# Dilated attention scores: from three split passes over both heads to one float32 matmul per head, and queries and keys written directly in class order

## The chip, the cores and the metric

The kernel runs on one core of a Trainium2 chip. The metric is the device time of one launch in microseconds (us). Before the change the median of three runs is 1536.92 us (1534.99 to 1537.64).

The engines are named as the profile names them: PE is TensorE's matmuls, PEld its weight loads, DVE is VectorE, ACT is ScalarE, POOL is GpSimd, SP is the queue from which nearly all DMAs are issued. PE writes its results to PSUM, which the program uses as eight banks of 128 x 512 float32; the other engines read them there. A line number such as L939 is a line of the kernel before, if nothing else is said.

## What is computed

An encoder block over 1024 tokens of width 1024: one input projection, three mixers side by side, a merge, an output projection. The change touches one mixer, the dilated window attention. It has 24 heads of width 64, in three groups `g` of eight heads; a group has a dilation `DIL[g]` of 1, 4 or 16.

```
def dilated_window_attention(q, k, v, window, dilation):
    half = window // (2 * dilation)          # 64, 64, 64
    qg, kg, vg = regroup(q), regroup(k), regroup(v)   # positions sorted by their class mod dilation
    ...
    sc = jnp.einsum('znqhd,znkhd->znhqk', qb, kw) * (dh ** -0.5)
    sc = jnp.where(valid[None, :, None], sc, NEG_INF)   # |qpos - kpos| <= 64, in the same class
    m = jnp.max(sc, axis=-1, keepdims=True)
    p = jnp.exp(sc - m)
    l = jnp.sum(p, axis=-1, keepdims=True)
    o = jnp.einsum('znhqk,znkhd->znqhd', p / l, vw)
    lse = m + jnp.log(l)
```

Queries and keys get rotary positions first. The outputs of the three groups are added up with weights softmax(lse).

## The kernel before

**Whole program.** PE's order is written out by hand. `weave` puts two streams together: the matmuls of dense projections (`dense`, 24 matmuls for half a unit of 128 output channels x 512 tokens, in three terms L143, L145, L147, because a float32 product is made from split operands: hi*hi, lo*hi, hi*lo), and the steps of an attention generator. After each step it goes on with the stream that is behind, by costs in ns that the code gives (216 for a dense matmul; an attention step yields its own). The totals that pace the attention are `A_COST`. On DVE, ACT, POOL and SP a scheduler sets the order from dependences and priorities; attention steps have the higher priority. An engine works off its queue in that fixed order.

**Stage of the dilated attention** (`with tc.tile_pool(name="aa")`). There are twelve visits, one for each head pair `p_` (0 to 3) and group `g` (0 to 2). Each visit (`a_att`) runs woven into three dense units: queries, keys and values of the visit after it (`add_a`). The last visit runs woven into three units of another stage. A unit's result comes in two halves in two PSUM tiles `d` (there are two such banks for the whole program), and has to be taken out of them before the half after next can start on PE.

Taking them out, for queries and keys (`rope_half`, L832 to L838): three DVE multiplications with the cosine and sine tables `tab` into `rot` and `t2a`, then one POOL addition. After the second half the keys or queries are split: `aqh` by ACT and `aql` by DVE for queries (L105, L106); for keys, one copy for each of the two heads in which the other head's rows are zero (`C_KM`), `akh` by ACT (L862) and `akl` by DVE (L863). The tokens are sorted into classes in these splits (`class_view`, `cls`). For values (L879) DVE writes the sorted classes at once, and POOL copies the class ends (L885).

**One visit**, with eight query tiles `T` of 128:

- transposes of the values (L913), brought to SBUF by ACT (L915)
- `scores(T)`: three matmuls (`passes`, L125) of one query tile against both heads' keys, the heads side by side in one PSUM bank (`s`, two banks); `n` is the key window, 128, 192 or 256 columns for a head. For each head DVE adds the mask and takes the minimum (L939), and ACT makes the exponential and its sum (L942 to L947)
- `trans(T)`: three, four or two transposes of the exponentials (L965, L974) into one PSUM tile `tr` (two banks), brought to SBUF by ACT (`app`, L977)
- `pv(b)`: for four tiles, the product with the values (L989), in plain float32, each head's 64 columns on its own half of the array's columns, into `ov` (two banks); ACT brings it out (`og`, L998)
- at the end the minima and sums are transposed and stored (`sts`, `sr`, `std`)

`scores(T)` is followed by `trans(T - 2)`, and `pv` comes three tiles behind. After the three groups of a head pair, `combine` makes the weights (`ceg`, `wgd`, `wgt`) and multiplies the three `og` by them (L1083); its five steps are called at given tiles of the next visits (`STEP_T`) and are placed behind that tile's last score operation on DVE (`issue_after`).

## Time and profile before

| | |
|---|---|
| median of 3 runs | 1536.92 us |
| profiled execution | 1537.39 us, span 1535.6 us |
| mean granted TensorE clock | 0.993 |
| PE, PEld busy | 1498.6, 1238.4 us |
| DVE, ACT, POOL busy | 972.8, 712.7, 443.9 us |
| stage of the dilated attention | 585 to 1151 us of the span: 566 us |
| in that stage PE, DVE, ACT, POOL busy | 563.1, 328.8, 282.9, 121.5 us |

An engine's busy time is the time in which at least one of its instructions runs. PE's matmuls overlap: a record of 0.39 us can start 0.23 us after the one before it, so PE's rate is read from the distance of starts. In a view by windows a row has, for each engine, the busy time and, behind it in brackets, the number of instructions, and then the granted clock, the DMA share and GB/s. In a view of groups a row has line, engine, operation, tiles, shape, count, then busy us and mean ns, then the idle time before it and who ended it.

### The profile page before, as it was taken

What the parts mean: (1) busy time and instruction counts of PE and PEld (TensorE: products, weight loads), DVE (VectorE), ACT (ScalarE), POOL (GpSimd) and SP (SyncE); (2) the same over time, 40 slices, a digit from 0 to 9 for tenths busy, and PEclk for the clock granted to TensorE, in tenths of its full rate; (3) what the DMA queues carried; (4) which work ended last, traced back from release to release, by engine and by line L of the source; (5) the groups of instructions that cost most, each with busy time, mean ns of one, the idle gap of its engine ahead of it and who ended that gap; (6) DMA issues with size and microseconds to landing.
All of it is one profiled execution on the core that took longest, in us unless ns stands there. A gap on an engine that the chain in (4) does not pass through costs nothing.

```text
span 1535.6 us, 20807 instructions
## 1 busy us (share of the span) xinstructions
PE 1498.6 (98%) x7748; PEld 1238.4 (81%) x7748; DVE 972.8 (63%) x1598; ACT 712.7 (46%) x1457; POOL 443.9 (29%) x363
## 2 busy tenths in 40 slices
PE   6999989999999999999999999999999999999998
PEld 5899977777777778888878888887888788888787
DVE  7765469989988985555566466556625442524843
ACT  5453346676666662554446445444642111212321
POOL 4415512444544552211221222122200100233422
PEclk9999999999999999999999999999999999999999
DMA  5332011111112112101121121112126441523332
GB/s 211 95 126 70 29 42 62 56 42 62 53 41 63 62 56 93 41 29 42 45 68 42 42 80 47 42 31 83 42 76 194 164 132 35 204 70 117 124 110 96
DMA packets 55044, 119.79 MB, mean 78 GB/s; under 512 B 13792, under 2 KB 23712, under 8 KB 54816
## 3 DMA queue, kind: packets, MB, share of 16 engines
q1 hardware_dynamic: 54800, 118.34, 23.4%
q8 instruction: 61, 1.00, 0.3%
q14 instruction: 39, 0.32, 0.1%
q10 hardware_dynamic: 144, 0.13, 0.0%
HBM read 96.06 MB, written 22.38 MB: 77 GB/s over the span
## 4 chain that ended last, share of the span: by engine, by line
PE 75%; DVE 11%; issue 4%; ACT 3%; DMA 3%; POOL 2%; SPq 0%; DVEq 0%; POOLq 0%; ACTq 0%
PE d L147 12%; PE d L143 12%; PE d L145 12%; PE sc L125 7%; PE sc L1248 4%; PE s L125 3%; PE sc L147 3%; PE sc L145 3%; PE sc L143 3%; PE ov L989 2%; DVE bpl L106 2%; PE s L709 1%; DVE bn L691 1%; PE ov L730 1%; PE s L708 1%
## 5 line engine op out<-in xcount | busy, mean ns | idle before, releaser
L143 PE MATMUL d<-hh,wh 128*128 128x512 f32 x992 | 396.1, 399 | 1.4 <-DVE fth L222 1.4
L147 PE MATMUL d<-hh,wl 128*128 128x512 f32 x992 | 397.2, 400 | 0.0
L145 PE MATMUL d<-hl,wh 128*128 128x512 f32 x992 | 393.6, 397 | 0.0
L147 PEld LDWEIGHTS d<-hh,wl 128*128 128x128 f32 x992 | 187.1, 189 | 38.5 <-issue 3.6
L143 PEld LDWEIGHTS d<-hh,wh 128*128 128x128 f32 x992 | 187.2, 189 | 38.3 <-DVE fth L222 2.3
L145 PEld LDWEIGHTS d<-hl,wh 128*128 128x128 f32 x992 | 187.1, 189 | 36.2 <-issue 1.0
L105 ACT ACTIVATE wh<-wr 128x1024 fp32r<-128x1024 f32 (+1 forms) x100 | 95.4, 955 | 246.7 <-PE sc L145 108.3
L720 POOL TENSOR_TENSOR bl<-bl,bp 128x512 f32<-128x512 f32 x96 | 135.5, 1412 | 120.4 <-ACT bp L711 112.1
L838 POOL TENSOR_TENSOR rot<-rot,t2a 128x512 f32<-128x512 f32 x48 | 82.6, 1721 | 297.4 <-DVE t2a L837 297.4
L106 DVE TENSOR_TENSOR bpl<-bp,bph 128x512 fp32r<-128x512 f32 x128 | 130.5, 1020 | 23.8 <-ACT bph L105 23.3
L106 DVE TENSOR_TENSOR wl<-wr,wh 128x1024 fp32r<-128x1024 f32 (+1 forms) x100 | 119.0, 1191 | 21.2 <-ACT wh L105 20.5
L1149 POOL TENSOR_TENSOR acc<-acc,th 128x1024 f32<-128x1024 f32 x16 | 45.4, 2837 | 203.8 <-DVE th L1148 203.8
L711 ACT ACTIVATE bp<-s 128x512 f32<-128x512 f32 x128 | 76.2, 595 | 60.0 <-PE s L709 58.2
L947 ACT ACTIVATE pra<-pra,sts 128x128 f32<-128x128 f32 (+2 forms) x152 | 67.2, 443 | 61.9 <-DVE sts L939 61.2
L147 PE MATMUL sc<-hh,wl 128*128 128x512 f32 x224 | 87.8, 392 | 1.8 <-DVE wl L106 1.8
L691 DVE TENSOR_REDUCE bn<-tr 128x1 f32<-128x512 f32 x128 | 86.7, 681 | 4.4 <-PE tr L690 3.9
L143 PE MATMUL sc<-hh,wh 128*128 128x512 f32 x224 | 87.9, 392 | 0.0
L145 PE MATMUL sc<-hl,wh 128*128 128x512 f32 x224 | 87.9, 392 | 0.0
L939 DVE CUSTOM_DVE_ANT_0 pra<-s,mask 128x128 f32<-128x128 f32 (+2 forms) x152 | 48.4, 348 | 61.8 <-PE s L125 49.1
L105 ACT ACTIVATE bph<-bp 128x512 fp32r<-128x512 f32 x128 | 80.9, 632 | 3.5
L835 DVE TENSOR_TENSOR rot<-d,tab 128x512 f32<-128x512 f32 x48 | 33.1, 690 | 67.5 <-PE d L147 67.2
L125 PE MATMUL sc<-gh,wh 128*128 128x512 f32 x192 | 74.7, 389 | 0.0
(278 smaller groups left out, 3096.9 us busy)
## 6 DMA issues: line engine op xcount, KB each, us to landing
wr<-in_wu SPq DMA_DIRECT2D x76, 512.0 KB
g2d<-fth SPq DMA_DIRECT2D x24, 256.0 KB
wgt<-wgd SPq DMA_DIRECT2D x24, 256.0 KB
ot<-od SPq DMA_DIRECT2D x12, 512.0 KB
gt<-g2d SPq DMA_DIRECT2D x12, 512.0 KB
wr<-in_wbr SPq DMA_DIRECT2D x24, 256.0 KB
thd<-fth SPq DMA_DIRECT2D x20, 256.0 KB
th<-thd SPq DMA_DIRECT2D x10, 512.0 KB
```

Source lines behind the costliest of these rows:

```text
L105: A.activation(dst_h, src, AF.Copy)
L106: V.tensor_tensor(dst_l, src, dst_h.bitcast(F32), op=OP.subtract)
L125: PE.matmul(out_ps, a, b, start=i == 0, stop=i == n - 1)
L143: PE.matmul(dst, wh[:, k, :], hh[k][:, t], start=k == 0, stop=False)
L145: PE.matmul(dst, wh[:, k, :], hl[k][:, t], start=False, stop=False)
L147: PE.matmul(dst, wl[:, k, :], hh[k][:, t], start=False, stop=k == 7)
L691: V.tensor_reduce(st[i]["n"][:, j, c:c + 1], s, axis=AX.X, op=OP.min)
L711: A.activation(pp, s, AF.Exp, scale=-1.0)
L720: G.tensor_tensor(lsum[i % 2], lsum[i % 2], pp, op=OP.add)
L838: G.tensor_tensor(o[:, t], o[:, t], t2, op=OP.add)
L947: A.activation(src, raw, AF.Exp, scale=-1.0, bias=bias, accum_out=sts[:, h, 1, T:T + 1])
L1248: PE.matmul(parts[h], *terms[h][j], start=j == 0, stop=j == 23)
```

## The change

1. The split and the zeroed copies of queries and keys go. `qk_evac` writes one float32 tile for queries (`aq`) and one for keys (`ak`), each with two buffers, already in class order: `rope_half` reads PSUM and tables through the strided view `classes`. The scale -0.125 goes into the query's multiplications (`scalar_tensor_tensor` in place of `tensor_tensor`).
2. The channel order of the weights is the plain one (`layout`), so the sine part of `rope_half` is four multiplications on 32 partitions, where there were two on 64.
3. `scores` is one float32 matmul for each head, on 64 rows of the array: head 0 on rows 0 to 63, head 1 on rows 64 to 127, each into its own PSUM bank. One call does four query tiles; a visit calls it twice.
4. PSUM: four banks for scores, one for `tr`, one for `ov` (before: two, two, two).
5. The order of the attention's steps: `scores(0)` first, then for each tile 300 ns of dense work and `trans(T)`; the second `scores` before tile 2, the first `pv` before tile 5. `A_COST` is new. The steps of `combine` are placed behind the last multiplication that takes a `d` tile out (`fp["last"]`).

```diff
-    phase_psum("ps_a", s1=2, t=2, o=2)
+    phase_psum("ps_a", s1=4, t=1, o=1)
...
+        def half_of(ap, half, g):
+
+            if g == 0:
+                return ap[:, half * 512:half * 512 + 512]
+            n = S // DIL[g] // 2
+            return ap.rearrange("p (r u) -> p r u", r=DIL[g])[:, :, half * n:half * n + n]
+
+        def classes(ap, g):
+            return ap if g == 0 else ap.rearrange("p (u r) -> p r u", r=DIL[g])
...
-        def rope_half(o, half, p):
+        def rope_half(o, half, p, scale, g):
             t = slice(half * 512, half * 512 + 512)
             t2 = aa.tile([P, 512], F32, name="t2a", bufs=2)
-            V.tensor_tensor(o[:, t], p, tab[:, 0, t], op=OP.mult)
-            V.tensor_tensor(t2[0:64], p[64:128], tab[64:128, 1, t], op=OP.mult)
-            V.tensor_tensor(t2[64:128], p[0:64], tab[0:64, 1, t], op=OP.mult)
-            G.tensor_tensor(o[:, t], o[:, t], t2, op=OP.add)
+            cos, sin = [classes(tab[:, i, t], g) for i in range(2)]
+            p = classes(p, g)
+            dst = half_of(o, half, g)
+            tmp = t2 if len(p.shape) == 2 else t2.rearrange("p (r u) -> p r u", r=DIL[g])
+
+            def mult(out, x, y):
+                if scale is None:
+                    return V.tensor_tensor(out, x, y, op=OP.mult)
+                return V.scalar_tensor_tensor(out, x, scale, y, op0=OP.mult, op1=OP.mult)
+
+            mult(dst, p, cos)
+            for a in range(4):
+                i, j = slice(32 * a, 32 * a + 32), slice(32 * (a ^ 1), 32 * (a ^ 1) + 32)
+                fp["last"] = mult(tmp[i], p[j], sin[j])
+            G.tensor_tensor(dst, dst, tmp, op=OP.add)
...
-            def q_evac(half, p):
...
-                if half == 1:
-                    d["q"] = (aa.tile([P, S], R, name="aqh", bufs=2), aa.tile([P, S], R, name="aql", bufs=2))
-                    split(cls(d["q"][0], g), cls(d["q"][1], g), class_view(d["rot"], g))
...
-                    for h in range(2):
-                        mc = cs[:, C_KM + h:C_KM + h + 1]
-                        A.activation(cls(kh[:, h], g), ov, AF.Copy, scale=mc)
-                        V.scalar_tensor_tensor(cls(kl[:, h], g), ov, mc, cls(kh[:, h], g).bitcast(F32),
-                                               op0=OP.mult, op1=OP.subtract)
+            def qk_evac(name, scale):
+                def evac(half, p):
+                    if half == 0:
+                        d[name] = aa.tile([P, S], F32, name=f"a{name}", bufs=2)
+                    rope_half(d[name], half, p, scale, g)
+                return evac
...
-            def scores(T):
-                lo, hi, mo = window(g, T)
-                n = hi - lo
-                sv = pss1().rearrange("p (h k) -> p h k", h=2)[:, :, :n]
-                qs = slice(T * 128, T * 128 + 128)
-                passes(sv, [(qh[:, qs], kh[:, :, lo:hi]), (qh[:, qs], kl[:, :, lo:hi]), (ql[:, qs], kh[:, :, lo:hi])])
-                pr = aa.tile([P, 512], F32, name="pra", bufs=4)
+            def scores(b):
+                svs, cost = [], 0
+                for j in range(4):
+                    T = 4 * b + j
+                    lo, hi, mo = window(g, T)
+                    n = hi - lo
+                    if j % 2 == 0:
+                        banks = [pss1(), pss1()]
+                    sv = [x[:, j % 2 * 256:j % 2 * 256 + n] for x in banks]
+                    for h in range(2):
+                        hs = slice(h * 64, h * 64 + 64)
+                        PE.matmul(sv[h], span(qa[hs], T * 128, T * 128 + 128, g), span(ka[hs], lo, hi, g),
+                                  start=True, stop=True)
+                    svs.append((T, n, mo, sv))
+                    cost += 4 * n / 2.4
+                for T, n, mo, sv in svs:
+                    pr = aa.tile([P, 512], F32, name="pra", bufs=6)
...
-            for T in range(NT + LA_P):
-                if T < NT:
-                    cost = scores(T)
-                    if todo and T == STEP_T[-len(todo)]:
-                        with tc.issue_after(last["dve"].ins):
-                            todo.pop(0)()
-                    yield cost
-                if 0 <= T - LA_T < NT:
-                    yield trans(T - LA_T)
-                if T >= LA_P and (T - LA_P) % 4 == 3:
-                    yield pv((T - LA_P) // 4)
+            yield scores(0)
+            for T in range(NT):
+                if todo and T == STEP_T[-len(todo)]:
+                    with tc.issue_after(fp["last"].ins):
+                        todo.pop(0)()
+                if T == 2:
+                    yield scores(1)
+                if T == 5:
+                    yield pv(0)
+                yield 300
+                yield trans(T)
+            yield 300
+            yield 300
+            yield pv(1)
...
-        A_COST = (13200.0, 11800.0, 8000.0)
+        A_COST = (15300.0, 14300.0, 10500.0)
...
-            units.append(unit(b + pair))
-            units.append(unit(1536 + b + pair))
-            units.append(unit(3072 + b + np.arange(128)))
+            units += [unit(1536 * j + b + np.arange(128)) for j in range(3)]
```

More of the change, by code (lines that the diff above doesn't have):

```diff
@@ L21 @@
 DIL = (1, 4, 16)
-C_ID, C_KM, C_GP, C_GM, C_BM, C_END = 0, 128, 130, 138, 146, 426
+C_ID, C_GP, C_GM, C_BM, C_END = 0, 130, 138, 146, 426
 B_COS, B_SIN, B_QN, B_QS, B_KN, B_KS = 0, 512, 170, 234, 298, 362
@@ L818, in block, with span @@
         G.tensor_tensor(tab[:, 1], tab[:, 1], rb, op=OP.mult)
-        def class_view(ap, g):
+        def half_of(ap, half, g):
             if g == 0:
-                return ap
-            return ap.rearrange("p (u r) -> p r u", r=DIL[g])
-        def cls(ap, g):
-            if g == 0:
-                return ap
-            return ap.rearrange("p (r u) -> p r u", r=DIL[g])
+                return ap[:, half * 512:half * 512 + 512]
[3 more added lines that the diff above has]
+            return ap if g == 0 else ap.rearrange("p (u r) -> p r u", r=DIL[g])
+        def span(ap, lo, hi, g):
+            return ap[:, lo:hi]
         OPS = {}
-        def rope_half(o, half, p):
+        def rope_half(o, half, p, scale, g):
             t = slice(half * 512, half * 512 + 512)
             t2 = aa.tile([P, 512], F32, name="t2a", bufs=2)
-            V.tensor_tensor(o[:, t], p, tab[:, 0, t], op=OP.mult)
-            V.tensor_tensor(t2[0:64], p[64:128], tab[64:128, 1, t], op=OP.mult)
-            V.tensor_tensor(t2[64:128], p[0:64], tab[0:64, 1, t], op=OP.mult)
-            G.tensor_tensor(o[:, t], o[:, t], t2, op=OP.add)
+            cos, sin = [classes(tab[:, i, t], g) for i in range(2)]
[11 more added lines that the diff above has]
+            G.tensor_tensor(dst, dst, tmp, op=OP.add)
         def add_a(p_, g):
@@ L842, in add_a @@
             d = OPS[p_, g] = {}
-            def q_evac(half, p):
-                if half == 0:
-                    d["rot"] = aa.tile([P, S], F32, name="rot", bufs=1)
-                rope_half(d["rot"], half, p)
-                if half == 1:
-                    d["q"] = (aa.tile([P, S], R, name="aqh", bufs=2), aa.tile([P, S], R, name="aql", bufs=2))
-                    split(cls(d["q"][0], g), cls(d["q"][1], g), class_view(d["rot"], g))
-            def k_evac(half, p):
-                if half == 0:
-                    d["rot"] = aa.tile([P, S], F32, name="rot", bufs=1)
-                rope_half(d["rot"], half, p)
-                if half == 1:
-                    kh = aa.tile([P, 2, S], R, name="akh", bufs=1)
-                    kl = aa.tile([P, 2, S], R, name="akl", bufs=1)
-                    ov = class_view(d["rot"], g)
-                    for h in range(2):
-                        mc = cs[:, C_KM + h:C_KM + h + 1]
-                        A.activation(cls(kh[:, h], g), ov, AF.Copy, scale=mc)
-                        V.scalar_tensor_tensor(cls(kl[:, h], g), ov, mc, cls(kh[:, h], g).bitcast(F32),
-                                               op0=OP.mult, op1=OP.subtract)
-                    d["k"] = (kh, kl)
+            def qk_evac(name, scale):
[4 more added lines that the diff above has]
+                return evac
             def v_evac(half, p):
@@ L878, in v_evac @@
                     p, rv = [v.rearrange("p (u r) -> p r u", r=r) for v in (p, rv)]
-                V.tensor_tensor(dst, p, rv, op=OP.mult)
+                fp["last"] = V.tensor_tensor(dst, p, rv, op=OP.mult)
                 if half == 1 and g < 2:
@@ L885, in v_evac @@
                             G.tensor_copy(vd[hs, e, :DIL[g], h], src)
-            units = [(base, q_evac), (base + 1, k_evac), (base + 2, v_evac)]
+            units = [(base, qk_evac("q", -0.125)), (base + 1, qk_evac("k", None)), (base + 2, v_evac)]
             for u, evac in units if base else units[::-1]:
@@ L893, in a_att @@
             d = OPS.pop((p_, g))
-            qh, ql = d["q"]
-            kh, kl = d["k"]
-            vt = d["vt"]
+            qa, ka, vt = d["q"], d["k"], d["vt"]
             for _ in range(4):
@@ L920, in a_att @@
             sts = cb.tile([P, 2, 2, NT], F32, name="sts", bufs=2)
-            st, last = {}, {}
+            st = {}
             def blocks_of(T):
@@ L925, in blocks_of @@
                 return [(i, c - lo, m) for i, (c, m) in enumerate(blocks) if lo <= c < hi]
-            def scores(T):
-                lo, hi, mo = window(g, T)
-                n = hi - lo
-                sv = pss1().rearrange("p (h k) -> p h k", h=2)[:, :, :n]
-                qs = slice(T * 128, T * 128 + 128)
-                passes(sv, [(qh[:, qs], kh[:, :, lo:hi]), (qh[:, qs], kl[:, :, lo:hi]), (ql[:, qs], kh[:, :, lo:hi])])
-                pr = aa.tile([P, 512], F32, name="pra", bufs=4)
-                for h in range(2):
-                    src = pr[:, h * n:h * n + n]
-                    bias = sts[:, h, 0, T:T + 1]
-                    moved = n == 192 and (h == 0) == (blocks_of(T)[0][2] == 64)
-                    raw = sv[:, h] if moved else src
-                    last["dve"] = V.tensor_tensor_reduce(raw, sv[:, h], mask[:, mo:mo + n], 1.0, 3.0e38, OP.add, OP.min, bias)
-                    if moved:
-                        a, b = (64, 0) if h == 0 else (0, 128)
-                        A.activation(src[:, h * 64:h * 64 + 128], raw[:, a:a + 128], AF.Exp, scale=-1.0, bias=bias,
-                                     accum_out=sts[:, h, 1, T:T + 1])
-                        A.activation(src[:, 128 - h * 128:192 - h * 128], raw[:, b:b + 64], AF.Exp, scale=-1.0, bias=bias,
-                                     accum_out=lx[:, h, T:T + 1])
-                    else:
-                        A.activation(src, raw, AF.Exp, scale=-1.0, bias=bias, accum_out=sts[:, h, 1, T:T + 1])
-                st[T] = pr
-                return 3 * n * 0.84
@@ new lines, in scores @@
+            def scores(b):
[15 more added lines that the diff above has]
+                    pr = aa.tile([P, 512], F32, name="pra", bufs=6)
+                    for h in range(2):
+                        src = pr[:, h * n:h * n + n]
+                        bias = sts[:, h, 0, T:T + 1]
+                        moved = n == 192 and (h == 0) == (blocks_of(T)[0][2] == 64)
+                        raw = sv[h] if moved else src
+                        V.tensor_tensor_reduce(raw, sv[h], mask[:, mo:mo + n], 1.0, 3.0e38, OP.add, OP.min, bias)
+                        if moved:
+                            a, c = (64, 0) if h == 0 else (0, 128)
+                            A.activation(src[:, h * 64:h * 64 + 128], raw[:, a:a + 128], AF.Exp, scale=-1.0, bias=bias,
+                                         accum_out=sts[:, h, 1, T:T + 1])
+                            A.activation(src[:, 128 - h * 128:192 - h * 128], raw[:, c:c + 64], AF.Exp, scale=-1.0,
+                                         bias=bias, accum_out=lx[:, h, T:T + 1])
+                        else:
+                            A.activation(src, raw, AF.Exp, scale=-1.0, bias=bias, accum_out=sts[:, h, 1, T:T + 1])
+                    st[T] = pr
+                return cost
@@ L1305, in unit @@
         return w[:, cols].reshape(8, P, 128).transpose(1, 0, 2)
-    i32 = np.arange(32)
-    pair = np.concatenate([i32, 64 + i32, 32 + i32, 96 + i32])
     units = []
@@ L1343, in layout @@
     r['msk'] = m
-    lane = np.arange(128) // 32 % 2
-    cst[:, C_KM] = np.where(lane == 0, -0.125, 0.0)
-    cst[:, C_KM + 1] = np.where(lane == 1, -0.125, 0.0)
     cst[:, C_GP:C_GP + 8] = inp['g_pre'][0].reshape(8, P).T
@@ L1361, in layout @@
         tab[q * 32:q * 32 + 32, 0] = ca.T
-        tab[q * 32:q * 32 + 32, 1] = sa.T if q < 2 else -sa.T
+        tab[q * 32:q * 32 + 32, 1] = -sa.T if q % 2 else sa.T
     r['tabA'] = tab
```

## The prediction

> **What bounds the kernel now.** The page first: PE is busy for 98% of the span, and PE's three dense lines lead the chain of work that ended last. The view by windows cuts out the stage that is changed; then the groups (every shape apart) and the timeline of that stage.

> ```profile
> PE 1498.6 (98%) x7748; PEld 1238.4 (81%) x7748; DVE 972.8 (63%) x1598; ACT 712.7 (46%) x1457; POOL 443.9 (29%) x363
> ...
> PE d L147 12%; PE d L143 12%; PE d L145 12%; PE sc L125 7%; PE sc L1248 4%; PE s L125 3%; PE sc L147 3%; PE sc L145 3%; PE sc L143 3%; PE ov L989 2%; DVE bpl L106 2%; PE s L709 1%; DVE bn L691 1%; PE ov L730 1%; PE s L708 1%
> ```

> ```profile
> 585.00:1151.00 566.00, 563.11 (x3180) 461.10 (x3179) 328.77 (x692) 282.85 (x698) 121.53 (x87) 1.00 0.17 53
> ```

> In 566 us PE idles 2.9. DVE (328.8 busy) and ACT (282.9) have room on average, but each works in order: it matters when they are late. Starts of PE in one piece of the timeline:

> ```profile
> 642.64 0.40 PE L143 MATMUL d<-hh,wh 128*128 128x512 f32 x1
> 642.97 1.97 PE L989 MATMUL ov<-app,avs 128*64 128x128 f32 x32
> 644.87 0.50 PE L145 MATMUL d<-hl,wh 128*128 128x512 f32 x1
> 645.21 0.40 PE L147 MATMUL d<-hh,wl 128*128 128x512 f32 x1
> ...
> 649.35 0.33 PE L125 MATMUL s<-akh,aqh 128*128 128x384 f32 x1
> 649.52 0.34 PE L125 MATMUL s<-akl,aqh 128*128 128x384 f32 x1
> ```

> The reader is to see the distances: dense matmuls stand 0.228 apart elsewhere in this stage, a 384-column score matmul costs 0.17, and the plain float32 product has two records for each matmul, and its 32 records start in 16 pairs, 0.109 a pair for 128 columns: the two heads, on two halves of the array, run at once. From 642.64 to 645.21 are 2.57 us; less two dense ones (0.456) and 16 x 0.109 (1.744), 0.37 is left for going into the split array and out.

> **The change, part by part**, against the profiled execution's 1537.4 (span 1535.6 and 1.8 around it; 0.5 over the median).

> *Scores on PE.* Before: 96 tiles x 3 passes at 0.23 (24 tiles of 512 columns), 0.173 (40 of 384), 0.116 (32 of 256): 48.6 us. After: the windows of one head sum to 24x256 + 40x192 + 32x128 = 17,920 columns; at the pair's rate, two passes of 0.109 per 128 columns for both heads, 30.5 us. 24 calls at 0.37 add 8.9. Row halves are nowhere in this trace; between both heads at once and one after the other I take at once, by the nearest row (the column halves), and for the switch the same row; the ends are 30.5 and 69.9. Net **-9.2**.

> *Removed copies.* `aqh`, `akh` take 63.6 off ACT, `aql`, `akl` 64.2 off DVE; nothing of it is on PE.

> *Taking queries and keys out of PSUM.* Five DVE operations for a half instead of three, and for g = 1, 2 strided. The values are already taken out so:

> ```profile
> L879 DVE TENSOR_TENSOR vta<-d,rb x24: 684/1063/1098, 586.2 to 1112.2; 128x512 f32<-128x512 f32 x24
> ```

> Its eight plain ones take 0.69, its sixteen strided ones 1.04 to 1.10. With 0.015 between operations (rope before: 0.705 from start to start at 0.69) a strided half costs 5 x 1.085 = **5.4 us** of DVE, a plain one 3.5; before it was 2.1. Sum: 16 x 3.5 + 32 x 5.4 - 48 x 2.1 = +128, less the 64 removed: DVE goes from 329 to some 393 in the stage. That scaling the query costs nothing more is by L222 (a scalar_tensor_tensor, 685 ns against 680). A half must be out before the half after next starts; a half is 5.5 us on PE, 7 with attention. So DVE is now just short of PE's pace and everything else in its queue pushes a half back. No row has 32 partitions strided: the ends are a plain 0.705 and 1.1; L836 on 64 partitions (693 ns), L835 on 128 (690) and L699 on 4 (689) cost the same, so I take 1.085.

> *POOL's additions* stay 48 at 1.28 to 2.33 us, 5.4 apart at the least: hidden. *Query scale in channels, constants*: nothing.

> *Bunched scores, one `tr` bank.* The order of the changed program on each engine says who stands behind whom. ACT: all exponentials of tiles 4 to 7, then `app` of tile 2. PE: the transposes of tile 3 need the only `tr` bank, hence that `app`. Before, exponentials came a tile at a time and there were two banks. I walk the three kinds of visit with the rows.

> Visit of g = 1 (queries and keys of g = 2 woven in), from the end of the queries' first half. DVE: hand-over 0.25, first half 5.4, eight L939 at 0.40 from start to start 3.2, second half 5.4, eight more 3.2, among them a weight split 1.35: 18.8; ACT's last exponentials and `app` 1.5: 20.3. PE until tile 3's transposes: 49 dense matmuls 11.2, two score calls 3.3, three transpose calls 1.3: 15.8. **PE waits 4.5.** For p_ >= 1 a multiplication by the weights (L1083, 2.02) stands in the same DVE stretch: 6.5 in two pieces (2.2 before the third tile of the second score call, whose banks tile 3 of the first still holds).

> Visit of g = 0: the same walk ends 0.7 late at the second half of the keys for p_ = 0. For p_ >= 1 ACT's `ceg` stands between the exponentials and `app`, and waits for DVE's small operations behind a weight split: 2.5 more, 3.2.

> Visit of g = 2: plain halves, 3.5 each, and L939 at 0.22: nothing.

> Sum 4.5 + 3 x 6.5 + 0.7 + 3 x 3.2 = **+34.3**. Off go three stalls of now (a transpose and a product waiting for `app`, 1.2 together per p_ >= 1): -3.5. If the cover were whole (0) or DVE slower, the ends are 0 and 45.

> *The clock.* A long wait costs once more:

> ```profile
> 1194.00:1195.00 1.00, 1.00 (x4) 0.76 (x5) 1.00 (x2) 0.00 (x0) 0.00 (x0) 0.63 0.28 41
> 1195.00:1196.00 1.00, 1.00 (x4) 0.81 (x3) 1.00 (x1) 0.00 (x0) 0.00 (x0) 0.50 0.88 348
> ```

> This follows PE starts 2.18 us apart (1191.65 to 1193.84); the clock (third number from the end) is 0.5 and the matmuls stand 0.43 apart for 3.4 us, 1.7 lost. A distance of 1.66 (at 419) cost nothing. I take 1.7 for each of the four waits over 4 us: **+6.8**; the three of 2.5 are too near the limit to count, ends 0 and 7 x 3.4. [...]

> *Moved steps.* `combine`'s DMAs go behind the last `d` multiplication: on SP a 512 KB weight load now stands before `wgd` instead of after the first `wgt`; it feeds a unit two ahead, and SP's own longest wait is for weight splits (158.6 us in this stage), so nothing, at most 1 us per head pair. `A_COST` equals the new steps' sum within 2%: attention and dense work still end together.

> Sum: 1537.4 - 9.2 - 3.5 + 34.3 + 6.8 = 1565.8, **1566**.

> **The rivals.** *Faster: DVE keeps up.* Place: the ten operations of two query halves in each g = 1 visit. If 32 partitions strided cost 0.705, that chain is 3.8 shorter, the waits shrink to 0.7 and 2.7, g = 0's to about 0, no clock is lost: 1537.4 - 9.2 - 3.5 + 8.8 = 1533.5, and 1525 if the switch costs nothing too. It decides below about 0.75 an operation. Against it: L879 has the same views.
> *Row halves one after the other.* Scores cost 30.5 more; in the visits of g = 1 (2.6 each) and three of g = 0 (1.6 of 3.3) that comes out of the waits: 1566 + 30.5 - 10.4 - 5 = 1581. For it: no row of this trace has two row halves at once.
> *Weight loads bind.* A score tile needs four loads of 128 columns. The 256-column passes show one such load per 0.116; four of these in a row are 0.46, against 0.22, 0.33, 0.44 by the pair's rate for 128, 192, 256 columns: 32 x 0.25 + 40 x 0.14 + 24 x 0.03 = 14.3, of it 4.5 inside g = 1's waits: 1576. [...] Against it: L989's loads start in pairs.
> *No change in work done*: not open, the copies are gone from the order.

> **How the numbers follow.** Forecast (1545 to 1580 by the ends of waits and clock) 0.50; DVE keeps up 0.25; row halves serial 0.13; weight loads 0.12. The range leaves out half of the fast case's lower part and little above: 1527 to 1586. A measurement of this kernel tells 0.2% (3 us) from no change. Slower: the three slow cases, less a little of the first, 0.72; within 0.2% 0.06; faster 0.22.

> **What the profile after would show.** DVE near 393 busy in the stage, strided 32-partition operations near 1070 ns; PE's score records in pairs, some 1.6 us a call for g = 0; PE waiting for ACT `app` once in each visit of g = 1; granted clock dipping there. Wrong if those operations are near 700 ns, if PE has no such waits, or if single score records follow one another at full length.

## The result and the profile after

The changed kernel takes 1559.68 us in the median of 4 runs (1557.76 to 1560.97), beside 1536.64 for the kernel before: 1.0156 times, so 1.6% slower, 95% interval 1.0144 to 1.0169. A second measurement (experiment 6) gave 1.0145 (1.0128 to 1.0163). The forecast was 1566, the range 1527 to 1586. The profiled execution took 1560.97 (span 1559.2) at a mean granted clock of 0.986. Line numbers from here on are those of the changed kernel; an experiment that adds lines has its own.

The page of the changed kernel, engines and the chain that ended last:

```profile
PE 1501.5 (96%) x7844; PEld 1226.9 (79%) x7844; DVE 1029.4 (66%) x1658; ACT 652.8 (42%) x1421; POOL 442.1 (28%) x363
...
PE d L143 12%; PE d L147 12%; PE d L145 12%; PE sc L125 7%; PE sc L1257 4%; DVE t2a L846 3%; PE sc L147 3%; PE sc L143 3%; PE sc L145 3%; PE ov L995 2%; DVE bpl L106 2%; PE ov L730 1%; PE s L709 1%; PE s L934 1%; PE s L708 1%
```

A new engine stands in the chain: DVE with `t2a`, the sine part of `rope_half`. The stage of the dilated attention (view by windows; columns as in the section on the profile before):

```profile
585.00:1175.00 590.00, 568.04 (x3284) 451.21 (x3283) 385.32 (x752) 223.90 (x662) 119.93 (x87) 0.98 0.17 51
```

ACT lost 59 us of work, DVE gained 57, and PE, which idled 2.9 us in 566, idles 22. The stage starts where it did, and the first matmul behind it, of tile `sc`, starts at 1175.38 in place of 1153.22: 22.2 us of the loss lie in the stage. From there to the end of the span are 383.8 us, 382.3 before; in experiment 6 they are 380.9, so this part differs from one execution to the next.

**What a score call costs PE** (timeline of PE, a call of g = 0):

```profile
618.79 0.47 PE L147 MATMUL d<-hh,wl 128*128 128x512 f32 x1
619.19 1.89 PE L934 MATMUL s<-ak,aq 64*128 64x192 f32 x16
621.01 0.50 PE L143 MATMUL d<-hh,wh 128*128 128x512 f32 x1
```

From the first of the 16 records to the next dense start are 1.82 us. The records start in pairs, 0.006 to 0.007 us apart, one of each head, and a pair of 256 columns takes 0.215 from start to start: both row halves work at once.

**What taking queries and keys out costs DVE** (the tile `t2a`; ns are least, median, greatest):

```profile
L845 DVE TENSOR_TENSOR t2a<-d,tab x96: 679/1021/1087, 597.9 to 1124.8; 32x512 f32<-32x512 f32 x96
L846 DVE SCALAR_TENSOR_TENSOR t2a<-d,tab x96: 679/1027/1100, 608.7 to 1106.8; 32x512 f32<-32x512 f32 x96
```

By group the medians are 687 ns (plain), 1057 (dilation 4) and 1022 (dilation 16). The values, with the same strided views, are where they were:

```profile
L877 DVE TENSOR_TENSOR vta<-d,rb x24: 691/1058/1084, 586.3 to 1134.7; 128x512 f32<-128x512 f32 x24
```

**Whom PE waits for** (view of waits, 580 to 1180; total us, times, longest):

```profile
PE tr L971 <- ACT app L983: 11.3, 5, 3.0
PE tr L980 <- ACT app L983: 8.2, 3, 2.7
PE d L143 <- DVE t2a L846: 1.8, 4, 0.5
```

Measured by the distances of PE's starts, these are 13 gaps with 23.7 us over the usual 0.23. Six of them are 3.1 to 3.4 us long, one in each visit of g = 0 and g = 1 with p_ >= 1. One of the kind in g = 1, in the timeline:

```profile
811.66 0.35 ACT L948 ACTIVATE pra<-s,sts 128x128 f32<-128x128 f32 x1
...
812.07 1.03 DVE L846 SCALAR_TENSOR_TENSOR t2a<-d,tab 32x512 f32<-32x512 f32 x1
...
813.09 0.40 PE L147 MATMUL d<-hh,wl 128*128 128x512 f32 x1
813.13 1.92 DVE L1092 TENSOR_TENSOR og<-og,wgt 128x1024 f32<-128x1024 f32 x1
...
815.08 0.36 DVE L945 CUSTOM_DVE_ANT_0 pra<-s,mask 128x192 f32<-128x192 f32 x1
...
815.48 0.45 ACT L953 ACTIVATE pra<-pra,sts 128x192 f32<-128x192 f32 x1 [2.01 <-DVE sts L945]
...
815.93 0.47 ACT L983 ACTIVATE app<-tr 128x384 f32<-128x384 f32 x1
...
816.46 0.90 PE L971 MATMUL tr<-cs,pra 128*128 128x128 f32 x3 [2.97 <-ACT app L983]
```

Read it from below. PE wants the transposes of tile 1; the only `tr` bank still holds tile 0. Its copy `app` was possible from 812 on, but ACT's queue has the exponentials of the four tiles ahead of it, all but those of the last head. The last of them waits 2.01 us for DVE's mask operation, and DVE is busy with a strided multiplication and then with `combine`'s weighting (L1092). So one PSUM bank ties PE to ACT's order, and that to DVE's. In the visits of g = 0 PE is held at tile 3's transposes, by the same bank and another delay of ACT:

```profile
772.28 2.31 DVE L106 TENSOR_TENSOR wl<-wr,wh 128x1024 fp32r<-128x1024 f32 x1
...
774.95 0.24 ACT L1077 ACTIVATE ceg<-ceg 128x48 f32<-128x48 f32 x1 [3.13 <-DVE ceg L1076]
775.10 0.58 ACT L983 ACTIVATE app<-tr 128x512 f32<-128x512 f32 x1
```

`ceg` waits on ACT for DVE's small operations behind a weight split, and `app` stands behind `ceg`.

**The clock** after the gap that began at 813.09 (view by windows, clock third from the end):

```profile
814.00:815.00 1.00, 0.00 (x0) 0.00 (x0) 1.00 (x1) 0.00 (x0) 1.00 (x1) 1.00 0.00 0
815.00:816.00 1.00, 0.00 (x0) 0.00 (x0) 0.97 (x6) 0.52 (x3) 1.00 (x1) 0.76 0.00 0
816.00:817.00 1.00, 0.54 (x3) 0.55 (x4) 0.99 (x2) 1.00 (x7) 1.00 (x2) 0.50 0.00 0
```

It stays at 0.50 until 822.3. The stage has five such periods, of 3.4 or 6.8 us, 23.9 in sum, which cost half of that, 12.0, at most: in 1.7 us of them PE still stood in a gap that is counted already.

The account: 1537.4 - 7.9 (scores, below) - 3.5 (stalls that are gone) + 23.7 + 12.0 = 1561.7; measured 1561.0. The agreement is closer than the account deserves: its terms make the stage 24.3 us longer, and the stage grew by 22.2. Of the 2.1 between, 0.9 are the 1.7 us at half clock that are counted twice, and 1.5 us were lost behind the stage, where the account has nothing.

### The profile page after: what moved, and what is told of

Same layout as the page of the kernel before. It is cut to its first block, busy times and chain, and to the rows that moved or that the text cites. A ratio compares the mean times of both kernels' runs of the same rounds, so it can differ in the third digit from the quotient of the medians.

```text
span 1559.2 us, 20894 instructions
## 1 busy us (share of the span) xinstructions
PE 1501.5 (96%) x7844; PEld 1226.9 (79%) x7844; DVE 1029.4 (66%) x1658; ACT 652.8 (42%) x1421; POOL 442.1 (28%) x363
## 4 chain that ended last, share of the span: by engine, by line
PE 75%; DVE 16%; issue 3%; ACT 3%; DMA 3%; POOL 1%; SPq 0%; DVEq 0%; POOLq 0%; ACTq 0%
PE d L143 12%; PE d L147 12%; PE d L145 12%; PE sc L125 7%; PE sc L1257 4%; DVE t2a L846 3%; PE sc L147 3%; PE sc L143 3%; PE sc L145 3%; PE ov L995 2%; DVE bpl L106 2%; PE ov L730 1%; PE s L709 1%; PE s L934 1%; PE s L708 1%
## 5 line engine op out<-in xcount | busy, mean ns | idle before, releaser
L143 PE MATMUL d<-hh,wh 128*128 128x512 f32 x992 | 400.5, 404 | 3.9 <-DVE t2a L846 1.8
L147 PE MATMUL d<-hh,wl 128*128 128x512 f32 x992 | 398.9, 402 | 0.0
L145 PE MATMUL d<-hl,wh 128*128 128x512 f32 x992 | 397.0, 400 | 0.0
L143 PEld LDWEIGHTS d<-hh,wh 128*128 128x128 f32 x992 | 188.5, 190 | 49.5 <-issue 4.2
L147 PEld LDWEIGHTS d<-hh,wl 128*128 128x128 f32 x992 | 188.8, 190 | 40.1 <-issue 2.7
L145 PEld LDWEIGHTS d<-hl,wh 128*128 128x128 f32 x992 | 188.4, 190 | 38.6 <-issue 2.4
L106 DVE TENSOR_TENSOR bpl<-bp,bph 128x512 fp32r<-128x512 f32 x128 | 130.4, 1019 | 23.8 <-ACT bph L105 23.3
L106 DVE TENSOR_TENSOR wl<-wr,wh 128x1024 fp32r<-128x1024 f32 (+1 forms) x100 | 118.6, 1187 | 21.2 <-ACT wh L105 20.5
L852 POOL TENSOR_TENSOR aq<-aq,t2a 128x512 f32<-128x512 f32 x24 | 40.9, 1704 | 217.0 <-DVE t2a L846 172.2
L147 PE MATMUL sc<-hh,wl 128*128 128x512 f32 x224 | 88.0, 393 | 2.7 <-DVE wl L106 2.7
L846 DVE SCALAR_TENSOR_TENSOR t2a<-d,tab 32x512 f32<-32x512 f32 x96 | 88.6, 923 | 1.7
L691 DVE TENSOR_REDUCE bn<-tr 128x1 f32<-128x512 f32 x128 | 86.6, 680 | 4.4 <-PE tr L690 3.9
L845 DVE TENSOR_TENSOR t2a<-d,tab 32x512 f32<-32x512 f32 x96 | 88.6, 923 | 1.3
L852 POOL TENSOR_TENSOR ak<-ak,t2a 128x512 f32<-128x512 f32 x24 | 43.3, 1806 | 158.4 <-DVE t2a L845 158.4
L143 PE MATMUL sc<-hh,wh 128*128 128x512 f32 x224 | 87.8, 392 | 0.0
L145 PE MATMUL sc<-hl,wh 128*128 128x512 f32 x224 | 87.8, 392 | 0.0
L983 ACT ACTIVATE app<-tr 128x384 f32<-128x384 f32 (+2 forms) x96 | 46.1, 480 | 96.5 <-PE tr L980 62.8
```

The costliest lines, as they stand in the source:

```text
L106: V.tensor_tensor(dst_l, src, dst_h.bitcast(F32), op=OP.subtract)
L143: PE.matmul(dst, wh[:, k, :], hh[k][:, t], start=k == 0, stop=False)
L145: PE.matmul(dst, wh[:, k, :], hl[k][:, t], start=False, stop=False)
L147: PE.matmul(dst, wl[:, k, :], hh[k][:, t], start=False, stop=k == 7)
L691: V.tensor_reduce(st[i]["n"][:, j, c:c + 1], s, axis=AX.X, op=OP.min)
L845: return V.tensor_tensor(out, x, y, op=OP.mult)
```

## The experiments

Each is the changed kernel with one edit, if nothing else is said. Ratios are to the kernel before on the same chip.

**1. One pool of two PSUM banks for `tr` and `ov`, instead of one bank each.**

```diff
-    phase_psum("ps_a", s1=4, t=1, o=1)
+    phase_psum("ps_a", s1=4, t=2, o=0)
...
-                ov = pso()
+                ov = pst().rearrange("p a b -> p (a b)")
```

> The changed kernel with two PSUM banks for the transposes, which the product with the values now shares; nothing else. Theory W: the lost time is PE waiting for the copies of transposed tiles (app), which stand in ACT's queue behind the bunched exponentials, and these at the end of a long DVE chain; a second bank only lets PE run one transpose call (about 2.1 us) further before it meets the same chain. So the 23 us of waits shrink to about 17 and some clock dips go: 1548 (1538 to 1552). Rival B, that the single bank is the cause: all waits for app and the 12 us of half clock go, 1527 to 1530.

Measured 1546.46, ratio 1.0082 (1.0065 to 1.0098). Waits of the changed order:

```profile
PE d L143 <- DVE t2a L845: 6.8, 3, 3.4
...
PE s L934 <- ACT pra L950: 3.0, 3, 1.0
```

The transposes' waits shrink from 19.5 to 3.6 us (L971 and L980 together), but PE now waits for the `d` tiles that DVE has not taken out, and for the exponentials themselves. The gaps still sum to 18.1. So the bank decides where PE waits, and DVE how long; of some 24 us lost, the bank alone gives back 11 by the ratios. (By the trace it is 5.6 in gaps and 8.6 in the clock, where 23.9 us at half speed became 6.8; the 3 us between the two accounts are not explained.)

**2. Plain views: no stride in `rope_half`.**

```diff
-            cos, sin = [classes(tab[:, i, t], g) for i in range(2)]
-            p = classes(p, g)
-            dst = half_of(o, half, g)
+            cos, sin = [tab[:, i, t] for i in range(2)]
+            dst = half_of(o, half, 0)
```

> The changed kernel with queries and keys taken out of PSUM through plain views in all three groups; the sorting into classes is left out, so queries and keys stand in the order of tokens. One transpose bank as in the changed kernel. Theory W: each strided DVE operation falls from about 1.07 to 0.69, the chain before the copies is 1.9 us shorter for a half, waits fall from 23 to about 4, no clock dips: 1529 (1526 to 1535). Rival B (the bank alone): the waits stay, 1557 to 1561.

The stage, by windows:

```profile
585.00:1165.00 580.00, 570.81 (x3353) 456.58 (x3352) 337.22 (x768) 229.16 (x668) 120.11 (x87) 1.00 0.18 57
```

Measured 1531.6, ratio 0.9982 (0.9973 to 0.9992): 26 us come back, all that the change had lost and a little more, with one `tr` bank, bunched scores and the split array still there. DVE is 337.2 us busy from 585 to 1165, the gaps sum to 9.8 (three of 1.94, three of 1.80), and no clock period at half speed lies in the stage. This kernel leaves out the sorting as a whole, in PSUM, in the tables and in what is written; it shows that the strided views together are what makes this change slower, and not yet which of them.

**3. The steps of `combine` later in the visit.**

```diff
-        STEP_T = (0, 2, 4, 6, 1)
+        STEP_T = (0, 5, 6, 7, 5)
```

> The changed kernel with the steps of the weighting of the last head pair put later in the visits (tiles 0, 5, 6, 7 of the visit of g = 0 and 5 of g = 1), where DVE waits for PE anyway. Theory W: the visits of p_ = 1 to 3 then behave like those of p_ = 0, which wait 0.6 (g = 0) and 2.7 (g = 1) instead of 3.5 and 3.1 and show no clock dips: 1561 - 3 x 2.9 - 3 x 0.5 - 12 = 1539 (1535 to 1545). Rival B (the bank alone): no change, 1557 to 1561.

Measured 1547.83, ratio 1.0090 (1.0075 to 1.0105): between the theories. The gaps over 3 us are gone, and with them four of the five clock periods, but the gaps still sum to 23.7, some of them now at the next visit's value transposes:

```profile
PE tr L971 <- ACT app L983: 8.7, 7, 1.8
...
PE tr L909 <- POOL vda L883: 4.4, 3, 1.5
PE tr L909 <- DVE sr L1032: 3.7, 3, 1.4
```

With DVE just short of PE's pace, its backlog is paid wherever the next consumer stands. What this edit gained is the clock: 12.0 - 1.7 = 10.3, and the ratios put 8.4 to 10.1 us between this run and the two measurements of the changed kernel. Moving `combine` took no waiting away, it only cut it into shorter pieces.

**4. Class tables: cosine and sine copied once into class order.** Eight copies on ACT at the start of the stage; PSUM is still read with a stride.

```diff
+        tabg = [tab]
+        for g in (1, 2):
+            tg = aa.tile([P, 2, S], F32, name=f"tab{g}")
+            for i in range(2):
+                for half in range(2):
+                    t = slice(half * 512, half * 512 + 512)
+                    A.activation(tg[:, i, t].rearrange("p (r u) -> p r u", r=DIL[g]),
+                                 tab[:, i, t].rearrange("p (u r) -> p r u", r=DIL[g]), AF.Copy)
+            tabg.append(tg)
...
-            cos, sin = [classes(tab[:, i, t], g) for i in range(2)]
+            cos, sin = [tabg[g][:, i, t] for i in range(2)]
+            if g:
+                cos, sin = [v.rearrange("p (r u) -> p r u", r=DIL[g]) for v in (cos, sin)]
```

> The changed kernel with the cosine and sine tables copied once into class order for g = 1 and 2, so that of the two inputs of each DVE multiplication only the PSUM one is strided. Both theories are silent on what a strided PSUM read alone costs. If the stride of either input makes the operation slow, it stays near 1.07 us and the time at 1560; if only the SBUF input's stride does, it falls to 0.69, and by theory W the time to that of plain views, about 1529.

Measured 1532.87, ratio 0.9990 (0.9981 to 1.0000), and the tile `t2a` reads

```profile
L856 DVE TENSOR_TENSOR t2a<-d,tab x96: 679/686/697, 596.7 to 1096.9; 32x512 f32<-32x512 f32 x96
```

One strided input, from PSUM, costs nothing: 686 ns at the median as in plain order. The same six gaps as in experiment 2 are left, 9.8 us. Whether it was the table's stride or two strides at once that cost, this run can't say; the next can.

**5. The mirror image: tables strided, PSUM plain.**

```diff
-            p = classes(p, g)
+            p = p if g == 0 else p.rearrange("p (r u) -> p r u", r=DIL[g])
```

> The mirror image of the class tables: the tables are read through the strided view, the PSUM result of the projection in token order (so queries and keys hold the wrong rotary positions and are not sorted into classes: that part of the computation is changed). Theory A (a strided read of SBUF is what costs, whatever PSUM does): operations of g = 1, 2 at 1010 to 1090 ns, all the waits of the changed kernel, 1.0145 to 1.0156 times the kernel before, about 1557 on a chip where that takes 1535. Theory B (only two strided inputs together cost, one is free): 686 ns and 0.999 times, about 1533. Theory C (each strided input costs a part): between 686 and 1010.

Measured 1557.68, ratio 1.0146 (1.0129 to 1.0163), the ratio of the changed kernel itself.

```profile
L845 DVE TENSOR_TENSOR t2a<-d,tab x96: 679/1021/1087, 596.8 to 1124.4; 32x512 f32<-32x512 f32 x96
```

Theory A holds: the stride in SBUF costs all of it, by itself.

**6. The changed kernel again**, for direct ratios beside the three runs that follow.

> The changed kernel once more, unchanged, beside the others on one chip, for direct ratios: 1.0156 to the kernel before, so 1557 to 1558 on a chip where that takes 1533.7.

Measured 1558.17, ratio 1.0145.

**7. Score calls of two query tiles**, on top of the class tables.

```diff
-                for j in range(4):
-                    T = 4 * b + j
+                for j in range(2):
+                    T = 2 * b + j
...
-                if T == 2:
-                    yield scores(1)
+                if T in (0, 1, 3):
+                    yield scores((T + 1) // 2 + 1)
```

> Class tables, and score calls of two query tiles instead of four: four calls a visit (at the start and before tiles 0, 1 and 3), so 24 more ways into and out of the row-split array. Theory of the sum (each call pays 0.37 us for the switch, whatever its size): the added calls cost 24 x 0.37 = 8.9 us; if the six waits of 9.8 us stay, 1541.8; if spreading the exponentials takes them all away, 1532. Rival (the switch costs nothing, the distance measured in four-tile calls is only the first fill): 1533 if the waits stay, 1523 if they go. The starts of the score records tell the two apart directly.

Measured 1538.88, ratio 1.0022 (1.0012 to 1.0031); the profiled span is 8.3 us longer than that of the class tables, of which 1.7 come from a period of half clock near the start of the program, outside the stage, that lasted 6.8 us and not 3.4. From the starts of PE: the calls take 40.0 us, where 24 larger ones took 35.3; before each call the distance is 0.33 (now and then 0.41) in place of 0.228, and after the first dense matmul behind it 0.34. Those two count 5.1 and 5.3 here, 2.7 and 2.7 there. So 24 more calls cost 50.4 - 40.7 = 9.7 us, 0.40 each, against 8.9 expected; the gaps shrank from 9.8 to 7.0 us. That makes 6.9 us, 8.6 with the 1.7, near the 8.3 of the two spans; the ratios, over all executions, say 4.9. The switch is real and the rival is out: bunching the scores saves it, and costs less in waits than it saves.

**8. All matmuls of head 0 first, then those of head 1**, on top of the class tables.

```diff
-                    for h in range(2):
-                        hs = slice(h * 64, h * 64 + 64)
-                        PE.matmul(sv[h], ...)
...
+                for h in range(2):
+                    hs = slice(h * 64, h * 64 + 64)
+                    for T, n, mo, sv in svs:
+                        lo, hi, _ = window(g, T)
+                        PE.matmul(sv[h], ...)
```

> Class tables, and in each score call the four matmuls of head 0 first and then the four of head 1, where before the heads alternated. Same work. Theory (two row halves run at once only when neighbours in PE's order use different halves): a call of g = 0, 1, 2 becomes some 1.5, 1.1 and 0.6 us longer (one head's share by the pair rate 0.109 per 128 columns and pass, less the one neighbouring pair in the middle), in sum some 26 us, of which a few go into the six waits there are: 1555 (1550 to 1560). Rival (the array keeps both halves busy by looking ahead in the queue): 1533, and the records still start in pairs.

Measured 1544.48, ratio 1.0059 (1.0043 to 1.0076), between the two. The first call, in PE's timeline:

```profile
617.54 2.75 PE L949 MATMUL s<-ak,aq 64*128 64x192 f32 x16
620.22 0.50 PE L143 MATMUL d<-hh,wh 128*128 128x512 f32 x1
```

2.68 us from its start to the next dense one, where alternating heads need 1.82; all calls together 53.0 in place of 35.3. That is 17.7, not 26: the first record of head 1 starts at 618.41, when head 0 has three of its eight still to start (618.62, 618.83, 619.05). PE brings work of the other row half forward, but only a few records. The gaps shrank by 4.4 at the same time, which leaves 13.3 us; the ratios say 10.6. So the order of the heads matters, and the changed kernel has the good one.

**9. Class tables and the two shared banks together** (the edits of experiments 4 and 1).

> The class tables of the run before, and the two PSUM banks of transposes and products shared by both (one pool of two instead of one bank each). With the class tables alone PE still loses 9.8 us in six gaps of 1.8 to 1.9 us at transposes of the visits with p_ >= 1, all waiting for the one tr bank. Theory (the transposes wait because the only tr bank is emptied by an app copy that stands behind exponentials in ACT's queue): with a second bank most of the six gaps go, 1532.9 - 8 = 1525 (1523 to 1529). Rival (the exponentials themselves are late behind the weighting steps of combine on DVE, so a second bank only moves the wait to the next transpose or to the scores): 1530 to 1534, and the gaps stay with another releaser.

Measured 1523.61, ratio 0.9919 (0.9906 to 0.9933): faster than both kernels, 34.6 us below the changed kernel on the same chip. PE's longest list of waits for ACT and DVE is down to

```profile
PE d L143 <- DVE t2a L856: 1.6, 2, 1.4
```

and the clock stays at 1.00 through the stage:

```profile
585.00:1150.00 565.00, 563.36 (x3322) 453.26 (x3321) 331.34 (x762) 232.65 (x673) 120.13 (x87) 1.00 0.18 55
```

The six gaps of 1.8 to 1.9 us are gone. One gap of 1.75 us is new, at 1045.14, where PE waits for DVE's `t2a`; so of the 9.8 us in gaps 8.3 came back and 1.5 moved. By the ratios of experiments 4 and 9 it is 10.9 us. With DVE ahead a second bank is worth most of what is lost there, where with DVE behind (experiment 1) it mostly moved the waits.

## Why the prediction was right, and where its sizes were off

**The bound and the sign were right**: DVE just short of PE's pace, PE waiting for `app` at a single `tr` bank. Experiment 2 takes all strides away, experiment 4 that of the tables alone, and the loss is gone; experiment 5 has only the tables' stride, and it is there again. The total is nearer than its parts: the waits came out 10.6 us smaller than forecast, the clock 5.2 and the scores 1.3 larger. That these errors partly cancel is luck.

**Scores on PE**: predicted 30.5 + 24 x 0.37 = 39.4, measured 35.3 + 2.7 + 2.7 = 40.7 at full clock (eight calls each of 1.82, 1.50 and 1.09 us, and the longer distances before and after). The switch is 0.42 a call, not 0.37: net -7.9 in place of -9.2.

**A strided operation at 1.085 us**: measured 1.079 and 1.035 from start to start at the median (dilation 4 and 16), 1 to 5% less; DVE 385 busy, predicted 393. The choice of L879 as the nearest row was right for a reason that I had not given: the two have a strided SBUF table in common. Partitions make little difference: the first of the five multiplications, on 128, takes 1.084 and 1.025 us at the median, the four on 32 take 1.057 and 1.022.

**PE's waits, 34.3**: this is the mis-sized term. Measured 23.7. g = 0 was nearly right (0.6 at p_ = 0, 3.5 at p_ >= 1, against 0.7 and 3.2), with the mechanism as written, `ceg` behind a weight split. For g = 1 I gave 4.5 and 6.5 and found 2.7 and 3.1. It bites one call earlier than I let it: at tile 1's transposes behind the exponentials of tiles 0 to 3, where I let the chain run to tile 3's, behind those of tiles 4 to 7. At p_ = 0 both are there, 1.9 us at tile 1 and 0.75 at tile 3. But this splits the wait and does not change its sum, because DVE works on almost without a pause from the first half to the last mask operation (views of DVE and of PE):

```profile
667.15 1.02 DVE L846 SCALAR_TENSOR_TENSOR aq<-d,tab 128x512 f32<-128x512 f32 x1 [4.60 <-PE d L147]
...
683.60 0.35 DVE L945 CUSTOM_DVE_ANT_0 s<-s,mask 128x192 f32<-128x192 f32 x1
...
685.33 0.55 PE L971 MATMUL tr<-cs,pra 128*128 128x128 f32 x3 [0.58 <-ACT app L983]
```

What was too large are the rows of the walk. From 667.15 to 683.95 are 16.8 us, where I had 18.55 for the same work (18.8 less the hand-over), mostly because mask operations of this visit stand 0.28 us apart at the median and I took 0.40; from there to PE's start are 1.4, not 1.5. These 1.9 us are the whole difference at p_ = 0. At p_ >= 1 they would leave 4.6, and PE waits 3.1 of it. The trace puts the rest down to the clock: PE at half speed falls back, so that DVE waits for its scores (0.47 us at 820.25) and PE for nothing at tile 3. Two other runs bear this out. In experiment 6 half clock follows the first gap at p_ = 0 too, and the gap at tile 3 is gone; in experiment 3 no half clock follows the first gap at p_ >= 1, and a gap of 0.95 to 0.97 us stands at tile 3. Waits and clock are not separate terms, as the sum has them.

**The clock, 6.8**: measured 12.0. I counted one period of 3.4 us for each of four waits over 4 us. The waits were shorter, but five of the six gaps of 3.1 to 3.4 us were followed by half clock, two of them for 6.8 us. The length of a gap alone does not decide: 3.12 us at 772.61 brought no half clock, 2.18 at 1191.65 in the kernel before did (last section). This error and the one before it are of opposite sign: 41.1 predicted for both together, 35.7 measured.

**Stalls of now, -3.5**: gone, as predicted. **POOL, SP, DMA**: no wait of PE for them appears, as predicted.

**The rivals.** *DVE keeps up* was priced at 1533.5, 3.9 below the profile before, and set to decide below 0.75 us an operation. The class tables fulfil its condition (0.686) by another way and give 0.9990, 1.5 us below: the rival's price was sound, and its condition was not met by this change. Its waits stand elsewhere than it said, 5.1 us in the visits of g = 0, where it had about 0, and 4.7 in those of g = 1, where it had 8.8. *Row halves one after the other* and *weight loads bind* fall by the pairs 0.006 us apart at 0.215 for 256 columns, and 1.09 us for a call of four 128-column tiles.

What stays open: the 2 and 3 us by which the ratios of experiments 7 and 8 differ from their accounts by the starts of PE, and the 3 us of experiment 1.

## What to carry to other kernels

Moving a sort from a copy into an operation that a critical engine does five times multiplies its stride by five (here DVE is 385 us busy in the stage, before 329); a constant operand can be sorted once instead (1.0156 became 0.9990 in experiment 4). A second buffer between two engines removes waits only while the slower one keeps up; before that it mostly moves them (experiment 9 got back 8.3 of 9.8 us in gaps, experiment 1 5.6 of 23.7), so first look for the engine that is late. Two matmuls on different halves of the array's rows should be neighbours in PE's order (the score calls took 35.3 us so, and 53.0 in experiment 8), and many of them in one go (0.40 us for each further call in experiment 7).

## What the runs showed of the hardware

**A stride in SBUF and one in PSUM were not alike for DVE.** By the medians of `t2a` a float32 multiplication of 512 columns on 32 partitions took 0.687 us with both inputs plain (the changed kernel, group 0), and 0.686 over all groups with only the PSUM input strided (experiment 4); with an SBUF table read 4 or 16 elements apart it took 1.057 or 1.022 (the changed kernel, where PSUM is strided too), and experiment 5, where only the table is strided, has the changed kernel's median over all groups, 1.021. For DVE's reads of PSUM no run here shows a cost of the stride.

**The clock doesn't go by the length of a gap alone.** A gap of 2.16 us at 674 in the changed kernel cost nothing; one of 2.18 at 676 in its second measurement, and one of 2.18 at 1191.65 in the kernel before, were followed by 3.4 us at half speed.

**PE started matmuls of another row half ahead of their turn** in experiment 8: in its first call a record of head 1 started at 618.41, before three records of head 0 (618.62, 618.83 and 619.05) that stand ahead of it in the program.
